# A hybrid decoder step on one core: gate and row loads on another queue, the merged sum added by an accumulating load, the last columns cut 384/160

## The chip, the core and the metric

One core of a Trainium2 chip runs the whole kernel. The metric is the device time of one execution in microseconds (us), the median of several runs. The profile is one execution taken by the hardware profiler; its times are us from the start of its span, unless marked ns. Engines: PE is TensorE (PEld its weight loads), DVE is VectorE, ACT is ScalarE, POOL is GpSimd, SP is the engine that does nothing here but issue DMAs. DMAs that ACT and POOL issue stand in those engines' own instruction order.

## What is computed

One layer of a decoder for 544 tokens (512 of a prompt, 32 of eight running requests). Three branches (short convolution, state-space, cross-attention) are projected to 2048 channels, gated, added and projected once more:

```
g = sigmoid(gpre).reshape(bsz, L, 3, D_MODEL)
conv_out = (cb * conv * silu(cz)) @ w_conv_out
ssm_out  = (ys @ w_glu_a) * sigmoid(ys @ w_glu_b)
attn_out = (o * silu(az)) @ w_attn_out
merged = g[:, :, 0] * conv_out + g[:, :, 1] * ssm_out + g[:, :, 2] * attn_out
y = rmsnorm(x + merged @ w_out) * final_norm_g
```

Everything is float32. Products are made in three matmuls of fp32r operands: each operand is split into a high part and a remainder, and hi·hi, hi·lo and lo·hi are accumulated.

## The kernel before

**Order.** The code is written for the Tile framework, whose planner puts each engine's instructions in an order by its own estimate of their times; so the order on an engine is not always that of the lines. Each engine then runs its list strictly in that order, and waits at the head of it.

**Weights.** A weight block of 512 KB (a "raw" tile) is loaded by SP. `split` makes its high part on ACT (L114, `whi`) and its remainder on DVE (L115, `wlo`), into a ring of pairs; the matmuls read the pair. `rings` sets the rings of a stage. `hold` is a tiny copy on POOL that reads the newest `wlo` (`ws["mark"]`) and writes the first element of a tile about to be loaded, so that the load is not issued earlier. `tick` runs one step of queued side work: first one entry of `later`, then steps of `bg`.

**Gate projections (to about 1546 us).** `winograd` makes products of the input projection by a seven-product scheme (order 1, 5, 6, 3, 7, 2, 4) from the factors `XT[1]` to `XT[7]` of the normed input, each 1088 KB for the high and 1088 KB for the low part. `XT[4]`, `XT[5]`, `XT[6]` are loaded by POOL at L1042 to L1044, right after the attention output has been stored by ACT (`od_d<-o_all`, L1031), and `XT[7]` at L1078. The first blocks of this stage's additional weight ring (`srw`) lie where `o_all` lay.

**Branch projections (about 1546 to 1917 us).** `winograd2` does the same for three output matrices with the factor sets `fsets` (`bh`, `bl`), four column groups `q` each: attention, convolution, then `w_glu_a` and `w_glu_b` in turn; 16 groups of seven products of 24 matmuls. Four raw tiles feed a group; `s1 = a21 + a22` (L1243, `bsum`) needs the third of them early. The ring of raw tiles has six slots (four `wraw`, two `bxr`), that of split pairs three. `gate` loads the group's two gate tiles (`sgate`, 544 KB each, two buffers) on SP, issued after the group's raw tiles. The gated results are stored by POOL to `mg_d` (L1285, L1296): the first branch plainly, the second and the third with an accumulating store that adds to what lies in DRAM.

**Handover and output projection (1917 us to the end).** Eight tiles `mgt` of the merged sum are read back by POOL (L1308) through two buffers, and split into 16 pairs `mh`, `ml` of 128 channels. The rows of x for the residual (`yt`, 4.46 MB in all) are loaded by POOL at the same place (L1325). Then seven column blocks of 256 go through `proj` (L172, L175, L178); after each, `residual` transposes the result on PE, adds it to `yt` (DVE), squares it (ACT) and multiplies by the norm's gain (POOL). The eighth block is made for tokens 0 to 271 first and then for 272 to 543 (L1381 to L1389), with `residual` and `finish` for row tiles 0, 1 and then 2, 3, 4. `finish` computes the norm, scales a row tile (2048 columns, on DVE or ACT) and stores it: two DMAs of SP for tiles 0 to 3, four of ACT for tile 4 (32 rows).

Of the kernel before, what the change touches and what calls it, by code (L numbers as in the profile page):

```python
# [7 lines left out]
F32 = mybir.dt.float32  # L8
# [19 lines left out]
def hybrid_step_kernel(  # L28
# [12 lines left out]
    with ctx:  # L41
# [1145 lines left out]

        frs = ExitStack()
        fsets = []
        for i in (1, 0):  # L1190
            pool = frs.enter_context(tc.tile_pool(name=f"fset{i}", bufs=1, side="right", reuse_waits="tile"))
# [19 lines left out]

        def winograd2(w, col0, F, before=None):

# [5 lines left out]
            a11, a12, a21, a22 = blk[0, 0], blk[0, 1], blk[1, 0], blk[1, 1]  # L1219
            if before:  # L1220
                before()

# [49 lines left out]
        def run(g):  # L1272
            for _ in g:
                pass

        rate[0] = 1
        for br, w, F, nxt in ((2, w_attn_out[0], fsets[0], 1), (0, w_conv_out[0], fsets[1], 2)):
            for q in range(4):
                o = winograd2(w, q * 512, F, (lambda: run(load_factors(F, fd[0], False))) if (br, q) == (2, 0) else None)
                if not q:  # L1280
                    bg.append(load_factors(fsets[nxt % 2], fd[nxt]))
                sg = gate(br, q)
# [15 lines left out]
        frs.close()  # L1298


        rings()
        open_std()
        mhp = ctx.enter_context(tc.tile_pool(name="mhp", bufs=1, side="right", reuse_waits="tile"))
        mh = [mhp.tile([128, T], F32R, name=f"mh{j}") for j in range(16)]
        ml = [mhp.tile([128, T], F32R, name=f"ml{j}") for j in range(16)]
# [5 lines left out]
        brs.close()  # L1311
        ytp = ctx.enter_context(tc.tile_pool(name="ytp", bufs=1, side="right", reuse_waits="tile"))
# [36 lines left out]

        def finish(tiles):  # L1350
            for i in tiles:
                rows = rows_of(i)
                ss = small.tile([128, 1], F32, name="ss")
                V.reduce_sum(out=ss[:rows], in_=ssp[:rows, i, :], axis=AX.X)
                r = rstd_of(ss, rows)
                if i % 2:
                    S.mul(yt[i][:rows], yt[i][:rows], r[:rows, 0:1])
                else:
                    V.tensor_scalar(yt[i][:rows], yt[i][:rows], r[:rows, 0:1], None, op0=ALU.mult)
                if i < 4:  # L1360
                    for s in range(2):
                        nc.sync.dma_start(out=yp_v[2 * i + s], in_=yt[i][64 * s:64 * s + 64])
                else:
                    for l in range(4):
                        S.dma_start(out=ys_o[l], in_=yt[i][8 * l:8 * l + 8])
# [11 lines left out]
        oT = [fin.tile([128, T], F32, name="oT", bufs=4) for _ in range(2)]  # L1377
        for n in range(2):
            for m in range(2):
                for blk, hi, lo in blocks:  # L1380
                    for q in range(4):  # L1381
                        kt = blk * 4 + q
                        lh = hi[:, q, m * 128:(m + 1) * 128]
                        ll = lo[:, q, m * 128:(m + 1) * 128]
                        o = ps[m][:, n, :NH]
                        nc.tensor.matmul(o, lh, mrh(kt, n), start=(kt == 0), stop=False)
                        nc.tensor.matmul(o, lh, mrl(kt, n), start=False, stop=False)
                        nc.tensor.matmul(o, ll, mrh(kt, n), start=False, stop=(kt == 15))
                (S.copy if m else V.tensor_copy)(oT[m][:, n * NH:(n + 1) * NH], ps[m][:, n, :NH])  # L1389
            tiles = ((0, 1), (2, 3, 4))[n]  # L1390
            residual(7, tiles, oT)
            finish(tiles)

# [33 lines left out]
```

## Time and profile before

| | us |
|---|---|
| median of 3 runs | 2165.47 |
| lowest, highest | 2164.09, 2172.06 |
| the profiled execution's own time | 2164.23 |
| span of its profile | 2161.8 |
| PE busy in the span | 2068.0 |
| DVE, ACT, POOL busy | 1284.9, 809.9, 439.5 |

The span is divided by its stages: what a stretch has in PE busy time, how many matmuls it holds, and which clock PE was granted. A PE busy share near 1 at a full clock cannot be shortened by moving loads; a stretch below it can. The profiled execution lasted 2.4 us longer than its span, and 1.2 us less than the median.

### The profile page before, as it was taken

To read this page: it belongs to the slowest core of one execution; us is meant where nothing else is said; L and a number is where in the kernel's file an instruction comes from. 1 tells how busy PE (TensorE), PEld (TensorE's weight loads), DVE (VectorE), ACT (ScalarE), POOL (GpSimd) and SP (SyncE) were. 2 spreads that over 40 slices of the span, in tenths; PEclk is the share of its full clock that TensorE was granted. 3 is DMA by queue.
4 is the path that set the end of the run, shared out by engine and by line. 5 is a ranking of instruction groups with operands and counts; after the bars stand their busy time and mean duration, and the time that the engine had idled before them with its cause. 6 is when DMAs were issued, how large, how long until landed. Compare 5 with 4: busy or idle time off the path is not lost.

```text
span 2161.8 us, 38757 instructions
## 1 busy us (share of the span) xinstructions
PE 2068.0 (96%) x16122; PEld 2016.1 (93%) x16122; DVE 1284.9 (59%) x1877; ACT 809.9 (37%) x1153; POOL 439.5 (20%) x518
## 2 busy tenths in 40 slices
PE   7999999999999999989999999999999899969996
PEld 5899999999999998879999999999899899969996
DVE  6664367943134743238887877767587686753232
ACT  6622222122122433224555555444444344433232
POOL 1008970054201102110121111000121100021121
PEclk9999999999999999999999999999999999989998
DMA  8747612234344626486677776643697955474223
GB/s 261 224 156 143 126 59 90 89 116 108 99 118 146 182 90 224 173 299 172 198 241 221 212 214 207 181 129 110 217 345 252 293 142 164 144 184 137 88 89 83
DMA packets 341619, 363.59 MB, mean 168 GB/s; under 512 B 62507, under 2 KB 288387, under 8 KB 338661
## 3 DMA queue, kind: packets, MB, share of 16 engines
q1 hardware_dynamic: 263712, 211.19, 33.2%
q0 software_dynamic: 38960, 118.48, 17.7%
q10 hardware_dynamic: 38772, 31.46, 5.0%
q8 instruction: 126, 2.06, 0.4%
q14 instruction: 49, 0.39, 0.1%
HBM read 280.82 MB, written 79.73 MB: 167 GB/s over the span
## 4 chain that ended last, share of the span: by engine, by line
PE 80%; DMA 7%; DVE 5%; POOL 2%; issue 2%; ACT 1%; ACTq 1%; DVEq 0%; SPq 0%; POOLq 0%
PE pA L1103 14%; PE pB L1103 11%; PE mmps L172 11%; PE mmps L178 11%; PE mmps L175 11%; PE pbA L1232 5%; PE pbB L1232 4%; DMA raw<-in_w_glu_b_dram 2%; DVE wlo L115 2%; DMA mgt<-mg_d 1%; PE mmps L324 1%; PE mmps L323 1%; PE mmps L325 1%; DMA raw<-in_w_in_dram 1%; DMA bl<-fd 1%
## 5 line engine op out<-in xcount | busy, mean ns | idle before, releaser
L115 DVE TENSOR_TENSOR wlo<-raw,whi 128x1024 fp32r<-128x1024 f32 x395 | 505.9, 1282 | 462.9 <-ACT whi L114 456.0
L114 ACT ACTIVATE whi<-raw 128x1024 fp32r<-128x1024 f32 x395 | 418.5, 1060 | 836.4 <-PE mmps L175 406.0
L172 PE MATMUL mmps<-xh,whi 128*128 128x272 f32 x1856 | 390.3, 291 | 1.5 <-ACT whi L114 1.3
L175 PE MATMUL mmps<-xl,whi 128*128 128x272 f32 x1856 | 389.6, 289 | 0.0
L178 PE MATMUL mmps<-xh,wlo 128*128 128x272 f32 x1856 | 386.7, 289 | 1.1 <-DVE wlo L115 1.1
L175 PEld LDWEIGHTS mmps<-xl,whi 128*128 128x128 f32 x1856 | 293.7, 188 | 4.3 <-issue 4.1
L172 PEld LDWEIGHTS mmps<-xh,whi 128*128 128x128 f32 x1856 | 290.9, 188 | 6.9 <-issue 4.5
L178 PEld LDWEIGHTS mmps<-xh,wlo 128*128 128x128 f32 x1856 | 290.9, 188 | 5.0 <-issue 2.7
L1232 PE MATMUL pbA<-bh,whi 128*128 128x272 f32 x512 | 149.5, 292 | 6.6 <-DVE bo L1256 5.0
L1232 PE MATMUL pbA<-bl,whi 128*128 128x272 f32 x512 | 149.1, 292 | 1.8 <-DMA bl<-fd 1.8
L1232 PE MATMUL pbA<-bh,wlo 128*128 128x272 f32 x512 | 148.9, 292 | 0.0
L1103 PE MATMUL pB<-xh,whi 128*128 128x272 f32 x432 | 126.2, 292 | 3.1 <-ACT whi L114 3.1
L1103 PE MATMUL pB<-xh,wlo 128*128 128x272 f32 x432 | 125.7, 291 | 0.0
L1232 PE MATMUL pbB<-bh,wlo 128*128 128x272 f32 x384 | 113.8, 296 | 12.0 <-DVE wlo L115 12.0
L1103 PE MATMUL pB<-xl,whi 128*128 128x272 f32 x432 | 125.3, 290 | 0.0
L1103 PE MATMUL pA<-xth,whi 128*128 128x272 f32 x432 | 124.4, 288 | 0.7 <-DVE sgate L1124 0.6
L1103 PE MATMUL pA<-xh,wlo 128*128 128x272 f32 x432 | 124.8, 289 | 0.0
L1103 PE MATMUL pA<-xh,whi 128*128 128x272 f32 x432 | 124.7, 289 | 0.0
L1103 PE MATMUL pA<-xth,wlo 128*128 128x272 f32 x432 | 124.6, 288 | 0.0
L1103 PE MATMUL pA<-xl,whi 128*128 128x272 f32 x432 | 124.4, 288 | 0.0
L1103 PE MATMUL pA<-xtl,whi 128*128 128x272 f32 x432 | 124.1, 287 | 0.0
L172 PE MATMUL mmps<-mh,whi 128*128 128x272 f32 x448 | 93.9, 294 | 21.0 <-ACT mh L114 21.0
(402 smaller groups left out, 4595.2 us busy)
## 6 DMA issues: line engine op xcount, KB each, us to landing
raw<-in_w_in_dram SPq DMA_DIRECT2D x224, 512.0 KB, 3.9
fd<-fs POOLq DMA_DIRECT2D x84, 272.0 KB, 4.0
raw<-in_w_out_dram SPq DMA_DIRECT2D x32, 512.0 KB, 3.4
gt_d<-sgate ACTq DMA_DIRECT2D x24, 544.0 KB, 3.1
sgate<-gt_d SPq DMA_DIRECT2D x24, 544.0 KB, 7.1
mg_d<-bo POOLq DMA_DIRECT2D x24, 544.0 KB, 8.4
bh<-fd POOLq DMA_DIRECT2D x21, 544.0 KB, 7.7
bl<-fd POOLq DMA_DIRECT2D x21, 544.0 KB, 9.0
```

Of the source, the lines that this page charges most:

```text
L114: S.activation(hi, src, AF.Copy)
L115: V.tensor_sub(lo, src, hi.bitcast(F32))
L172: nc.tensor.matmul(ps[m][:, n, :NH], lh, rh(kt, n), start=(kt == 0), stop=False)
L175: nc.tensor.matmul(ps[m][:, n, :NH], lh, rl(kt, n), start=False, stop=False)
L178: nc.tensor.matmul(ps[m][:, n, :NH], ll, rh(kt, n), start=False, stop=(kt == nk - 1))
L323: nc.tensor.matmul(o, lh, hi[:, q, :], start=(kt == 0), stop=False)
L324: nc.tensor.matmul(o, lh, lo[:, q, :], start=False, stop=False)
L325: nc.tensor.matmul(o, ll, hi[:, q, :], start=False, stop=(kt == 15))
L1103: nc.tensor.matmul(ps, a[:, k, :], t[:, k, :], start=new and i == 0, stop=i == 23, skip_group_check=not new)
L1232: nc.tensor.matmul(ps[:, s], a[:, k, s * 128:(s + 1) * 128], t[:, k, :], start=new and i == 0, stop=i == 11, skip_group_check=not new)
```

## The change

Five edits. The input factors are loaded as 5, 6, then 7 (as soon as its place is free), then 4, the last one held until the newest weight split. The gate tiles are loaded by POOL ahead of the group, no longer by SP behind its weights. The two `mgt` buffers are dropped and the raw ring of the branch projections gets two more slots, eight in all. The third branch is no longer stored: an accumulating load adds `mg_d` into the result tile in SBUF, and the split into `mh`, `ml` follows in later ticks, into memory of the factor set that is no longer used; the last tile is split after the last group. The row loads come after the first column block, and each `residual` runs one block later. The last column block is made for tokens 0 to 383 first, then for 160; `finish` follows for tiles 0, 1, 2 and then 3, 4, these scaled in two halves, one on DVE and one on ACT, and tile 3 stored in halves.

```diff
-        for n in (5, 6, 4):
+        def load_xt(n):
             for hl in range(2):
                 P.dma_start(out=XT[n][hl], in_=xf_d[n][hl])
+        load_xt(5)
+        load_xt(6)
...
-        for hl in range(2):
-            P.dma_start(out=XT[7][hl], in_=xf_d[7][hl])
+        load_xt(7)
+        for t in XT[4]:
+            hold(t[:, 0, 0:1])
+        load_xt(4)
...
-        mtp = brs.enter_context(tc.tile_pool(name="mgt", bufs=2, reuse_waits="tile"))
-        bxr = bps.enter_context(tc.tile_pool(name="bxr", bufs=2, reuse_waits="tile"))
-        rings([bxr] * 2, [bxh])
+        bxr = bps.enter_context(tc.tile_pool(name="bxr", bufs=4, reuse_waits="tile"))
+        rings([bxr] * 4, [bxh])
...
             for i in range(2):
-                nc.sync.dma_start(out=sg[i], in_=gt_d[br, 2 * q + i])
+                P.dma_start(out=sg[i], in_=gt_d[br, 2 * q + i])
...
-                o = winograd2(w, q * 512, F, (lambda: run(load_factors(F, fd[0], False))) if (br, q) == (2, 0) else None)
+                if (br, q) == (2, 0):
+                    for _ in load_factors(F, fd[0], False):
+                        pass
+                sg = gate(br, q)
+                o = winograd2(w, q * 512, F)
...
+        mh, ml = [], []
+        for pair in fsets[1].values():
+            for t in pair:
+                t = t.rearrange("p k t -> p (k t)")
+                mh.append(t[:, :T])
+                ml.append(t[:, T:])
+        def merged(t, k0):
+            for j in range(2):
+                split(mh[k0 + j], ml[k0 + j], t[:, j])
         for q in range(4):
+            sg = gate(1, q)
             o = winograd2(w_glu_a[0], q * 512, fsets[0])
-            sg = gate(1, q)
...
-                P.dma_start(out=mg_d[2 * q + i], in_=o[i], accum_op=ALU.add)
+                P.dma_start(out=o[i], in_=mg_d[2 * q + i], accum_op=ALU.add)
+                if (q, i) != (3, 1):
+                    later.append(lambda t=o[i], k0=4 * q + 2 * i: merged(t, k0))
+        flush()
+        merged(o[1], 14)
...
-        for i in range(8):
-            t = mtp.tile([128, 2, T], F32, name="mgt")
-            P.dma_start(out=t, in_=mg_d[i])
-            for j in range(2):
-                split(mh[2 * i + j], ml[2 * i + j], t[:, j])
...
-        for i in range(5):
-            hold(yt[i][:, 0:1])
-            load_rows(yt[i], i, P)
...
-            residual(jp, range(5), oT)
+            if not jp:
+                for i in range(5):
+                    hold(yt[i][:, 0:1])
+                    load_rows(yt[i], i, P)
+            else:
+                residual(jp - 1, range(5), prev)
+            prev = oT
+        residual(6, range(5), prev)
...
-        for n in range(2):
+        for n, (c0, c1) in enumerate(((0, 384), (384, T))):
...
-            tiles = ((0, 1), (2, 3, 4))[n]
-            residual(7, tiles, oT)
-            finish(tiles)
+            if n:
+                residual(7, (3, 4), oT)
+                finish((3, 4), True)
+            else:
+                residual(7, (0, 1, 2), oT)
+                finish((0, 1, 2))
```

## Rows read from the trace of the kernel before

**Rows 1.** The page's first line and the clock that PE was granted, in 40 equal slices of the span (tenths of full speed).

```profile
span 2161.8 us, 38757 instructions
PEclk9999999999999999999999999999999999989998
```

**Rows 2.** Busy time in six stretches. Columns: stretch, its length, then for PE, PEld, DVE, ACT and POOL the busy us (and instructions), the granted clock as a share of full speed, the DMA engines' busy share, GB/s.

```profile
1566.00:1676.00 110.00, 110.00 (x881) 110.00 (x880) 90.28 (x84) 48.22 (x56) 21.76 (x50) 1.00 0.91 301
1676.00:1917.00 241.00, 223.58 (x1709) 221.84 (x1707) 172.42 (x161) 102.49 (x118) 21.14 (x39) 0.96 0.60 178
1917.00:1962.00 45.00, 24.40 (x170) 23.16 (x171) 15.77 (x20) 14.20 (x22) 9.77 (x17) 0.81 0.94 245
1962.00:2117.00 155.00, 154.80 (x1238) 154.17 (x1237) 45.73 (x59) 48.24 (x101) 28.12 (x30) 1.00 0.25 84
2117.00:2143.00 26.00, 25.98 (x210) 25.65 (x207) 6.26 (x22) 8.03 (x21) 5.00 (x7) 1.00 0.13 30
2143.00:2162.00 19.00, 0.55 (x3) 0.27 (x3) 6.17 (x23) 3.81 (x11) 2.08 (x3) 0.60 0.69 194
```

**Rows 3.** PE's waits over the span: who waited for whom, us in total, times, longest.

```profile
PE mmps L172 <- ACT mh L114: 21.0, 4, 16.9
PE pbB L1232 <- DVE wlo L115: 12.0, 5, 4.0
PE pB L1103 <- ACT whi L114: 11.8, 5, 8.7
PE pbA L1232 <- DVE bo L1256: 5.0, 2, 4.4
```

**Rows 4.** What SP's own queue waited for from 1676 to 1917 us: us in total, times, longest.

```profile
SPq L1217 <- DVE wlo L115: 139.5, 34, 10.5
SPq L1269 <- DVE bo L1295: 27.1, 6, 8.3
SPq L1269 <- DVE bo L1284: 19.5, 6, 6.1
```

**Rows 5.** DVE's waits from 1545 to 1920 us, in the same columns.

```profile
DVE bsum L1243 <- DMA raw<-in_w_glu_b_dram: 25.1, 4, 7.7
```

**Rows 6.** SP's queue in order of time around the second `w_glu_b` group: start, us, what.

```profile
1768.89 2.53 SPq L1217 DMA_DIRECT2D raw<-in_w_glu_b_dram  x2
1779.80 0.34 SPq L1269 DMA_DIRECT2D sgate<-gt_d  x1
1780.93 0.37 SPq L1217 DMA_DIRECT2D raw<-in_w_glu_b_dram  x1
...
1786.08 0.37 SPq L1217 DMA_DIRECT2D raw<-in_w_glu_b_dram  x1
```

**Rows 7.** Instructions in order of time at the end of the first `w_glu_b` group: ACT's copy of the group's last product, and POOL's two accumulating stores.

```profile
1778.75 0.59 ACT L1262 COPY bo<-pbA 128x544 f32<-128x544 f32 x1
...
1780.06 0.85 POOL L1296 DMA_DIRECT2D mg_d<-bo  x1 [40.94 <-DVE bo L1295]
1782.40 0.85 POOL L1296 DMA_DIRECT2D mg_d<-bo  x1 [1.49 <-DVE bo L1295]
```

**Rows 8.** Those two stores, and the two around the handover (1910 to 1930 us): issues with KB each and us from issue to landing, then the least, median and greatest landing time of the handover's.

```profile
mg_d<-bo POOLq DMA_DIRECT2D x1, 544.0 KB, 8.4
mg_d<-bo POOLq DMA_DIRECT2D x1, 544.0 KB, 10.2
DMA to landing us min/median/max: 14.7/18.1/18.5
```

**Rows 9.** DVE's groups by shape from 1676 to 1917 us, and the remainders of the merged sum from 1917 to 1965 us: busy us, mean ns of one, idle before.

```profile
L115 DVE TENSOR_TENSOR wlo<-raw,whi 128x1024 fp32r<-128x1024 f32 x51 | 62.3, 1221 | 16.0 <-ACT whi L114 16.0
L1247 DVE TENSOR_TENSOR raw<-raw 128x1024 f32<-128x1024 f32 x9 | 11.0, 1219 | 0.0
L1256 DVE TENSOR_TENSOR bo<-pbA,bo 128x544 f32<-128x544 f32 x10 | 7.2, 721 | 4.2 <-PE pbA L1232 4.2
L1295 DVE TENSOR_TENSOR bo<-bo,sgate 128x1088 f32<-128x1088 f32 x7 | 9.0, 1286 | 1.2 <-ACT bo L1294 1.2
L115 DVE TENSOR_TENSOR ml<-mgt,mh 128x544 fp32r<-128x544 f32 x16 | 10.8, 722 | 26.4 <-ACT mh L114 26.4
```

**Rows 10.** ACT in order of time at the handover, and two groups of DMA issues from 1917 to 1962 us (KB each, median us to landing).

```profile
1941.44 1.20 ACT L114 ACTIVATE mh<-mgt 128x544 fp32r<-128x544 f32 x2 [15.34 <-DMA mgt<-mg_d]
...
yt<-in_x_prompt_dram POOLq DMA_DIRECT2D x3, 512.0 KB, 18.8
```

**Rows 11.** The input factors: SP's waits from 925 to 1005 us, and the landing times (least, median, greatest) of the three high and the three low loads of L1044.

```profile
SPq L1090 <- DMA od_d<-o_all: 21.3, 4, 12.1
...
DMA to landing us min/median/max: 7.2/13.8/19.9
...
DMA to landing us min/median/max: 9.9/16.8/23.0
```

**Rows 12.** Matmuls of other widths. Two of 512 columns in order of time (nine starts apart), four transposes of 128 columns in the chain that ended last, and a group of 72 columns in plain float32 (busy us, mean ns).

```profile
59.77 0.39 PE L324 MATMUL mmps<-wlo,mth 128*128 128x512 f32 x1
...
61.81 0.39 PE L324 MATMUL mmps<-wlo,mth 128*128 128x512 f32 x1
...
2117.01 0.44 PE aux L1342 x4
...
L717 PE MATMUL aux<-Sb,pw 128*128 128x72 f32 x128 | 28.3, 310 | 0.0
```

**Rows 13.** The end, in order of time: the first store of an output tile, the scaling of tile 2 (DVE) and of tile 3 (ACT), the four stores of tile 4 (ACT), and the DMA total from 2134 to 2162 us.

```profile
2138.53 1.17 SPq L1362 DMA_DIRECT2D out_dram<-yt  x2
...
2147.07 1.28 DVE L1359 TENSOR_SCALAR yt<-yt,rstd 128x2048 f32<-128x2048 f32 x1
2147.23 2.00 ACT L1357 ACTIVATE yt<-yt,rstd 128x2048 f32<-128x2048 f32 x1 [1.32 <-DVE rstd L216]
2149.99 6.99 ACTq L1365 DMA_DIRECT2D out_dram<-yt  x4
...
DMA packets 704, 4.46 MB, mean 159 GB/s; under 512 B 160, under 2 KB 160, under 8 KB 160
```

More of the change, by code (lines that the diff above doesn't have):

```diff
@@ L1184, in hybrid_step_kernel @@
         xs.close()
-        frs = ExitStack()
+        frs = [ExitStack(), ExitStack()]
+        ctx.callback(frs[1].close)
         fsets = []
         for i in (1, 0):
-            pool = frs.enter_context(tc.tile_pool(name=f"fset{i}", bufs=1, side="right", reuse_waits="tile"))
+            pool = frs[i].enter_context(tc.tile_pool(name=f"fset{i}", bufs=1, side="right", reuse_waits="tile"))
             fsets.insert(0, {n: tuple(pool.tile([128, 4, NH], F32R, name=f"b{hl}{n}_{i}") for hl in "hl")
                              for n in (4, 2, 7, 3, 6, 5, 1)})
-        mtp = brs.enter_context(tc.tile_pool(name="mgt", bufs=2, reuse_waits="tile"))
         bps = ExitStack()
@@ L1210, in load_factors, with winograd2 @@
                 yield
-        def winograd2(w, col0, F, before=None):
+        def winograd2(w, col0, F):
             blk = {}
@@ L1219, in winograd2 @@
             a11, a12, a21, a22 = blk[0, 0], blk[0, 1], blk[1, 0], blk[1, 1]
-            if before:
-                before()
             def product(ps, n, src, new):
@@ L1268, in gate @@
             for i in range(2):
-                nc.sync.dma_start(out=sg[i], in_=gt_d[br, 2 * q + i])
+                P.dma_start(out=sg[i], in_=gt_d[br, 2 * q + i])
             return sg
-        def run(g):
-            for _ in g:
-                pass
         rate[0] = 1
@@ L1278, in hybrid_step_kernel @@
             for q in range(4):
-                o = winograd2(w, q * 512, F, (lambda: run(load_factors(F, fd[0], False))) if (br, q) == (2, 0) else None)
+                if (br, q) == (2, 0):
[3 more added lines that the diff above has]
+                o = winograd2(w, q * 512, F)
                 if not q:
                     bg.append(load_factors(fsets[nxt % 2], fd[nxt]))
-                sg = gate(br, q)
                 for i in range(2):
@@ L1295, in hybrid_step_kernel @@
                 V.tensor_mul(o[i], o[i], sg[i])
-                P.dma_start(out=mg_d[2 * q + i], in_=o[i], accum_op=ALU.add)
+                P.dma_start(out=o[i], in_=mg_d[2 * q + i], accum_op=ALU.add)
+                if (q, i) != (3, 1):
+                    later.append(lambda t=o[i], k0=4 * q + 2 * i: merged(t, k0))
+        frs[0].close()
+        mhx = ctx.enter_context(tc.tile_pool(name="mhx", bufs=2, side="right", reuse_waits="tile"))
+        for j in range(2):
+            mh.append(mhx.tile([128, T], F32R, name="mhx"))
+            ml.append(mhx.tile([128, T], F32R, name="mlx"))
+        flush()
+        merged(o[1], 14)
         bps.close()
-        frs.close()
+        brs.close()
         rings()
         open_std()
-        mhp = ctx.enter_context(tc.tile_pool(name="mhp", bufs=1, side="right", reuse_waits="tile"))
-        mh = [mhp.tile([128, T], F32R, name=f"mh{j}") for j in range(16)]
-        ml = [mhp.tile([128, T], F32R, name=f"ml{j}") for j in range(16)]
-        for i in range(8):
-            t = mtp.tile([128, 2, T], F32, name="mgt")
-            P.dma_start(out=t, in_=mg_d[i])
-            for j in range(2):
-                split(mh[2 * i + j], ml[2 * i + j], t[:, j])
-        brs.close()
         ytp = ctx.enter_context(tc.tile_pool(name="ytp", bufs=1, side="right", reuse_waits="tile"))
@@ L1348, in residual, with finish @@
                 P.tensor_mul(yv, yv, fg[:rows, jp * 256:(jp + 1) * 256])
-        def finish(tiles):
+        def finish(tiles, halves=False):
+            rs = {}
             for i in tiles:
@@ L1354, in finish @@
                 V.reduce_sum(out=ss[:rows], in_=ssp[:rows, i, :], axis=AX.X)
[L1355 to L1363, printed above, removed]
+                rs[i] = rstd_of(ss, rows)
+            for i in tiles:
+                rows, r = rows_of(i), rs[i]
+                y = yt[i][:rows]
+                h = D // 2 if halves else D
+                for c, on_act in (((0, False), (h, True)) if halves else ((0, i % 2),)):
+                    if on_act:
+                        S.mul(y[:, c:c + h], y[:, c:c + h], r[:rows, 0:1])
+                    else:
+                        V.tensor_scalar(y[:, c:c + h], y[:, c:c + h], r[:rows, 0:1], None, op0=ALU.mult)
+                    if i < 4:
+                        for s in range(2):
+                            nc.sync.dma_start(out=yp_v[2 * i + s][:, c:c + h], in_=y[64 * s:64 * s + 64, c:c + h])
+                if i == 4:
                     for l in range(4):
-                        S.dma_start(out=ys_o[l], in_=yt[i][8 * l:8 * l + 8])
+                        S.dma_start(out=ys_o[l], in_=y[8 * l:8 * l + 8])
         for jp in range(7):
@@ L1377, in hybrid_step_kernel @@
         oT = [fin.tile([128, T], F32, name="oT", bufs=4) for _ in range(2)]
-        for n in range(2):
+        for n, (c0, c1) in enumerate(((0, 384), (384, T))):
             for m in range(2):
+                o = ps[m][:, n, :c1 - c0]
                 for blk, hi, lo in blocks:
@@ L1384, in hybrid_step_kernel @@
                         ll = lo[:, q, m * 128:(m + 1) * 128]
[L1385 to L1389, printed above, removed]
-            tiles = ((0, 1), (2, 3, 4))[n]
-            residual(7, tiles, oT)
-            finish(tiles)
+                        nc.tensor.matmul(o, lh, mh[kt][:, c0:c1], start=(kt == 0), stop=False)
+                        nc.tensor.matmul(o, lh, ml[kt][:, c0:c1], start=False, stop=False)
+                        nc.tensor.matmul(o, ll, mh[kt][:, c0:c1], start=False, stop=(kt == 15))
+                (S.copy if m else V.tensor_copy)(oT[m][:, c0:c1], o)
+            if n:
+                residual(7, (3, 4), oT)
+                finish((3, 4), True)
+            else:
+                residual(7, (0, 1, 2), oT)
+                finish((0, 1, 2))
 _INS = ['x_prompt', 'x_sample', 'mem_prompt', 'cache_mem_k', 'cache_mem_v', 'state_conv',
```

## The prediction

> **What bounds the kernel now.** I read the page first: over most of the span PE is granted its full clock, and the weak slices lie near the end [rows 1]. Then the stretches: from 1566 to 1676 us PE has work all the time, 881 matmuls in 110.0 us, 0.1249 us each, and again from 1962 to 2143 us. Two stretches fall short [rows 2]. From 1676 to 1917 us 1709 matmuls would take 213.4 us at that price; they take 241.0, so 27.6 us are lost, 17.4 of them as idle time and 10.2 to the lower granted clock (0.96 on average, so part of it at 1.2 GHz) that follows the gaps. From 1917 to 1962 us 170 matmuls would take 21.2 us and take 45.0: 23.8 us lost. After PE's last column block, 19 us of output follow. So the kernel is bound by PE, with 51.4 us that are someone else's.
>
> Whose, the waits tell. In the first stretch PE waits for DVE's weight remainders and for a copy [rows 3]; DVE in turn sat before `bsum`, 25.1 us for `w_glu_b` blocks alone [rows 5]; and those were late because SP had not issued them: its queue stood 46.6 us before gate loads whose buffers were still in use [rows 4]. The order of time shows it: two blocks of the next group go out at 1768.89, then SP stands before a gate load until 1779.80, and the third and fourth blocks follow at 1780.93 and 1786.08 [rows 6]. The 139.5 us before L1217 is a full ring of raw tiles, which is no loss by itself. In the second stretch PE waits 21.0 us for the merged sum's split [rows 3], ACT 15.34 us at once for an `mgt` load, which shares the DMA engines with the row loads (18.8 us to land) [rows 10].
>
> **The change part by part.**
>
> *Gate loads to POOL, eight raw slots.* The 24 gate issues leave SP, and with them all of the 46.6 us; a whole group of weights can lie ready. POOL takes them at about 0.85 us each [rows 7], 20 us in all, beside 21.14 busy us in a stretch of 241 [rows 2]. On POOL a gate load waits for the same release that the store of the last result waits for, so what is queued behind it (factor loads with their holds, the next store) loses little; the gate is used a group, 21 us, later. Removed: the 27.6 us. From below the bound is nothing, if DMA bandwidth and not the queue made the blocks late. I take the full removal, because the DMA engines are busy 0.60 of this stretch, against 0.91 in the one before it, where PE had no gap [rows 2].
>
> The Trainium skill speaks against this part: "DMA: Bandwidth & Descriptors", section "Issuing engines are not separate DMA queues", says that transfers run on the same 16 engines whichever engine issues them, so that spreading them only saves sequencer time. By that this term would be 0; the rows show a queue standing in order, not a shortage of engines. It is the second rival below.
>
> *Accumulating load and merged split in the ticks.* The load into SBUF stands in place of the accumulating store, which landed 8.4 and 10.2 us after issue [rows 8]. No row shows one into SBUF; I take those two, the nearest in kind, size and place. Above, the crowded handover's 18.5 us is the bound [rows 8]; below, nothing excludes that it lands at once, and then the stalls are none. New is a wait on ACT: the merged split stands in ACT's list between weight splits, and the next weight split is queued behind it, which PE waits for. Let T be the end of a group. The two loads go out at T+1.3 and T+3.7 [rows 7]. The second lands at T+13.9; two copies on ACT (1.2 us), then a weight split on ACT (about 1.1) and DVE (1.2), put the next weights at T+17.4, or T+landing+7.2. A product is 24 matmuls, 3.0 us; the sixth is due at T+15. That is a stall of 2.4 us; a landing of 8.4 us would make it 0.6. The copies of the first load stand in the way as well, so I take 2 us at each of the three transitions. DVE adds: a group has 7 splits of 1.22, 4 sums of 1.22, 3 additions of 0.72 and 2 gate products of 1.29 us, 18.2 us; four remainders of 0.72 make 21.1 in a group of 21.0 us [rows 9]. DVE is then full in three groups; I put 2 us on that in all. Stalls of 8 us; each idle us cost 0.59 us more by the clock in this stretch (10.2 over 17.4), so 12.7 us come back. Net: 27.6 - 12.7 = 14.9 saved. Bounds: 27.6, and 0 if every transition stalls 5 us.
>
> The same page, section "Anatomy of one DMA", has a fit of 2.0 us plus bytes over 436 GB/s, an estimate of 3.3 us for 544 KB; by it no merged split would be late and the sum would be some 10 us better. The stores measured 8.4 and 10.2, so it is not used.
>
> *Handover.* The eight `mgt` loads and 12 of the 16 splits leave it; the row loads move behind the first column block, where DMA is 0.25 busy and their first use is 25 us later [rows 2]. What is late next: the merged pairs 12 to 15. They belong to the fourth weight block of the first column block, due 18 us after the start; the loads land 10 to 14 us after it. The cost is again ACT's order: the third weight block may stand behind a merged split, some 2 us by the sum above, and 2 us for the start. Loss stood to idle time as 23.8 to 20.6 here, 1.16 [rows 2], so I keep 4.6 us and save 23.8 - 4.6 = 19.2; bounds 12 and 23.
>
> *Input factors.* The first blocks of the gate stage wait for the stores of `o_all`, whose place they take: SP stood 21.3 us for them [rows 11]. Those stores share the engines with POOL's loads. The new order sends 5, 6 and 7 at once and only then 4; the loads landed between 7.2 and 23.0 us after issue [rows 11], so number 7 is still under way when number 4 is released and POOL's queue never runs dry. The stores get the same share as now. I take 0; at best 3 us of the 8.7 us wait [rows 3], at worst 1. Behind the hold nothing urgent is queued on POOL.
>
> *Last block and tail.* 512 columns cost 0.227 us, nine starts in 2.04 us [rows 12], 272 cost 0.125, so 384 cost 0.173 by the line between them. 160 columns would be 0.077 by that line, but four transposes of 128 take 0.44, 0.11 each [rows 12]: I take 0.11, the row nearest in width. First part 96 × 0.173 = 16.6, second 96 × 0.11 = 10.6: 27.2 instead of 24.0 us. PE's end is not the end, though. Stores start at 2138.53 [rows 13], 8.5 us after the first part. The first part ends 4.6 us later than now, so stores begin near 2143.1; 4.46 MB at about 280 GB/s (they ran from 2138.5 to 2160 with gaps) take 15.9 us, so they end near 2159 to 2161, as before. The second part ends near 2146, its tile is scaled 6 us later in halves (0.65 on DVE, 1.0 on ACT instead of 2.00 [rows 13]), and its 1.3 MB join a stream still running. I take 0, from -3 to +3. The lagged residual moves 20 transposes per block by 25 us, past nothing that is short: PE has no idle time there [rows 2].
>
> **The sum.** 14.9 + 19.2 + 0 + 0 = 34.1 saved. From the profiled execution's 2164.2 that is 2130.1; against the median (1.2 higher) 2131. I say 2130.
>
> **The rivals.**
>
> *The merged load lands late (0.14).* At 12 us, each of four transitions stalls 12 - 7.8 = 4.2 us: 3 × 4.2 × 1.59 = 20.0, DVE 3.2, handover 7.2, in all 30.4 of the 51.4 come back: 2143. For it: no row has such a load; against it: without SP's burst behind each gate load these moments are emptier.
>
> *Queue order was not the cause (0.07).* If the blocks are late because the engines are shared, the first stretch keeps its loss, and only the handover gains: 2164.2 - 19.2 = 2145.
>
> *Narrow matmuls are dear (0.10).* The 72-column group took 28.3 us for 128, 0.22 each, in plain float32 and from strided data [rows 12]; by its price per column 160 columns would cost 0.49. Halfway, at 0.27 to 0.30, the second part takes 27 us, 16 more, of which stores hide 3: 2143.
>
> *Slower than before (0.05).* The merged load again, at its worst: each us of landing over 7.8 costs 3 × 1.59 + 1.16 = 5.9 us over the four transitions. With 5.5 fixed, the 51.4 saved are gone at a landing of 15.5 us, and 10.8 more at 17.4. The crowded handover had 14.7 to 18.5 [rows 8]; at 18.5 us it gives 2182. Against it: that crowd was the row loads, which move away.
>
> *It does not do what it says (0.04).* The planner's order may put the gate loads late on POOL, or merged splits before most weight splits, so that the old waits return under new names: about 2158.
>
> **How the numbers follow.** The forecast has 0.60. If nearly all of the 51.4 us goes and the tail and factors gain 3 us each at most, and a little stalls, the low end is 2112. The high end takes in three rivals with their spread: 2152. Left out are the last two rivals and the edges, about 0.15. A measurement here can tell about 0.5%, 10.8 us. Forecast and the first three rivals are faster by more than that, less a part of the first: 0.89. Within it: 0.07. Slower: 0.04.
>
> **What would show it.** SP's queue should have no wait for a gate's release, and `bsum` no wait for a block. From the convolution groups on, PE idle under 10 us. ACT waits for the accumulating loads, if they are late, stand at the first products of the second, third and fourth `w_glu_a` group. The handover's first `proj` should run within 5 us of full pace. The 160-column matmuls should start every 0.11 us. I am wrong if these loads land above 12 us, if PE's idle time is replaced by waits for DVE, or if the stores end over 3 us later after PE than I have them.

## The result, and the profile after

The changed kernel takes 2113.03 us (median of 4 runs, 2109.7 to 2114.6), the kernel before 2165.24 beside it: a ratio of 0.975, 95% interval 0.9726 to 0.9775. 52 us are gone where the forecast had 34: the direction was right, the size 17 us short of the 2130. By the medians the time is 1 us above the low end of the range (2112); by the ratio, from the 2165.47 that the prediction started from, it is 2111.3, just below it. The profiled execution took 2109.7 us, its span is 2107.8. The experiments below were timed in four rounds, each beside the kernel before, whose medians there lie between 2163.87 and 2166.03; so a difference between kernels of two rounds is good to some 2 us.

The title's "another queue" holds for the gate loads alone: the row loads stay on POOL and go out later. It leaves out two edits that turn out to pay, the two raw slots and the order of the input factors.

The page after: its first line, the granted clock in 40 slices, and the head of the chain that ended last; the weak slices of [rows 1] are gone but for the last.

```profile
span 2107.8 us, 38720 instructions
PEclk9999999999999999999999999999999999999998
...
PE 82%; DMA 5%; issue 5%; POOL 3%; DVE 3%; ACTq 1%; ACT 1%; POOLq 0%; SPq 0%; DVEq 0%
```

Stretches of the kernel after, in the columns of [rows 2]: the branch groups, the handover, the last block, the rest of the output.

```profile
1669.00:1886.00 217.00, 215.56 (x1719) 215.02 (x1718) 181.20 (x173) 110.11 (x131) 24.26 (x41) 1.00 0.63 188
1886.00:1931.00 45.00, 45.00 (x361) 45.00 (x361) 13.47 (x13) 12.59 (x16) 8.98 (x19) 1.00 0.93 233
...
2059.00:2089.00 30.00, 30.00 (x217) 29.75 (x215) 10.05 (x35) 10.45 (x33) 9.20 (x13) 1.00 0.06 13
2089.00:2108.00 19.00, 0.88 (x6) 0.32 (x5) 4.02 (x16) 3.79 (x9) 1.39 (x2) 0.60 0.74 216
```

In the branch groups PE idles 1.4 us where 17.4 were idle, and its clock is full; in the handover it idles not at all. Waits of the kernel after, from 1545 to 1920 us, that answer to [rows 3 to 5] (us in total, times, longest): PE's largest, then SP's own queue, then DVE's longest for a block.

```profile
PE pbA L1236 <- DVE wlo L115: 1.3, 1, 1.3
...
SPq L1223 <- DVE wlo L115: 250.8, 52, 12.4
...
DVE bsum L1247 <- DMA raw<-in_w_glu_a_dram: 6.1, 1, 6.1
```

The waits for a gate's release are gone from SP's queue. That fits the prediction, and is not the cause, as E2, E6 and E13 show.

**Where the time went** is read from three starts in each trace: that of the last matmul into `pB` (end of the gate projections), of the last into `pbA` (end of the branches), and of the first of the last column block. Before: 1542.8, 1916.3, 2117.2, span end 2161.8. After: 1535.7, 1884.3, 2059.5, 2107.8. The differences give four stretches (us), which every experiment has too (its time is the median of its own runs):

| kernel | time, us | to end of projections | branches | handover and 7 blocks | last block and output |
|---|---|---|---|---|---|
| before | 2165.24 | 1542.8 | 373.5 | 200.9 | 44.6 |
| after | 2113.03 | 1535.7 | 348.6 | 175.2 | 48.3 |
| E1 before, new input order | 2155.44 | 1540.0 | 372.9 | 199.3 | 44.4 |
| E2 before, gates on POOL | 2163.41 | 1546.8 | 374.8 | 201.1 | 44.5 |
| E3 after, old input order | 2121.93 | 1543.6 | 348.6 | 175.2 | 48.4 |
| E4 after, 272/272 | 2111.85 | 1536.0 | 350.9 | 175.2 | 45.5 |
| E5 after, six slots | 2137.86 | 1537.1 | 376.7 | 175.2 | 48.1 |
| E6 after, gates on SP | 2115.12 | 1538.3 | 353.9 | 175.2 | 47.6 |
| E7 after, merge twice | 2132.17 | 1538.2 | 356.9 | 185.2 | 48.7 |
| E8 after, store and reload | 2147.56 | 1537.9 | 350.5 | 210.6 | 48.3 |
| E9 before, wider rows | 2174.63 | 1546.2 | 379.4 | 204.3 | 44.5 |
| E10 after, wider rows | 2116.14 | 1540.9 | 347.9 | 175.2 | 47.9 |
| E11 after, wider rows for 6 | 2110.79 | 1536.7 | 348.1 | 175.2 | 48.5 |
| E12 after, row loads early | 2121.83 | 1535.4 | 347.7 | 184.4 | 48.5 |
| E13 before, eight slots | 2146.84 | 1544.9 | 348.4 | 208.8 | 45.0 |
| E14 after, seven slots | 2116.28 | 1538.7 | 352.4 | 175.2 | 48.5 |
| E15 E11, 272/272, halves | 2107.05 | 1536.6 | 349.5 | 175.1 | 44.3 |

The first stretch scatters by up to 4 us between profiles of kernels that do the same there (1542.8, 1546.8 and 1544.9 in before, E2 and E13), most of it ahead of the first input load, which goes out at 938.9 us in before and between 940.4 and 943.0 in all the others. From before to after the four give -7.1, -24.9, -25.7 and +3.7: -54.0, the difference of the two spans. The forecast had 0, -14.9, -19.2 and 0.

### The profile page after: what moved, and what is told of

The parts are those of the page before. It is cut to its first block, busy times and chain, and to the rows that moved or that the text cites. A ratio compares the mean times of both kernels' runs of the same rounds, so it can differ in the third digit from the quotient of the medians.

```text
span 2107.8 us, 38720 instructions
## 1 busy us (share of the span) xinstructions
PE 2056.4 (98%) x16122; PEld 2006.9 (95%) x16122; DVE 1284.3 (61%) x1878; ACT 809.3 (38%) x1154; POOL 447.1 (21%) x536
## 4 chain that ended last, share of the span: by engine, by line
PE 82%; DMA 5%; issue 5%; POOL 3%; DVE 3%; ACTq 1%; ACT 1%; POOLq 0%; SPq 0%; DVEq 0%
PE pA L1109 12%; PE mmps L172 12%; PE mmps L178 12%; PE mmps L175 12%; PE pB L1109 10%; PE pbA L1236 8%; PE pbB L1236 5%; DVE wlo L115 1%; DMA bl<-fd 1%; PE mmps L324 1%; PE mmps L323 1%; PE mmps L325 1%; DMA raw<-in_w_glu_a_dram 1%; PE aux L717 1%; DMA raw<-in_w_in_dram 1%
## 5 line engine op out<-in xcount | busy, mean ns | idle before, releaser
L1236 PE MATMUL pbB<-bl,whi 128*128 128x272 f32 x384 | 110.7, 288 | 1.2 <-DMA bl<-fd 1.2
```

The lines of the kernel that those rows point to most:

```text
L1236: nc.tensor.matmul(ps[:, s], a[:, k, s * 128:(s + 1) * 128], t[:, k, :], start=new and i == 0, stop=i == 11, skip_group_check=not new)
```

## Experiments on the branches: queue or slots

**E2, the gate loads alone.** The kernel before with

```diff
-                nc.sync.dma_start(out=sg[i], in_=gt_d[br, 2 * q + i])
+                P.dma_start(out=sg[i], in_=gt_d[br, 2 * q + i])
```

and `sg = gate(...)` ahead of the group's weights.

> The kernel before with the gate loads issued by POOL ahead of their group's weights; the ring of raw tiles stays at six slots, and the merged sum stays an accumulating store that is loaded again at the handover. Theory of the queue (SP standing before gate loads was the whole loss of the stage): the time between the last gate projection and the last branch matmul falls by 20 to 25 us, to about 2142. Rival, the two more ring slots did it: a gain under 8 us, 2157 or more, with waits of bsum for raw blocks left. Rival, shared engines (the queue that issues does not matter): no gain, 2164.

2163.41 us, ratio 0.9985 (0.997 to 1.0001); the branches take 374.8 us, as before. The prediction's queue theory falls. Waits of E2, SP's queue and DVE, from 1545 to 1920 us, and three instructions around one `w_glu_b` group in order of time: the remainder that freed a slot, SP's issue of the group's third block into it, and the sum that waited for that block.

```profile
SPq L1217 <- DVE wlo L115: 314.8, 58, 15.2
...
DVE bsum L1243 <- DMA raw<-in_w_glu_b_dram: 25.1, 4, 6.9
...
1784.71 1.22 DVE L115 TENSOR_TENSOR wlo<-raw,whi 128x1024 fp32r<-128x1024 f32 x1
...
1785.96 0.37 SPq L1217 DMA_DIRECT2D raw<-in_w_glu_b_dram  x1
...
1796.91 1.23 DVE L1243 TENSOR_TENSOR bsum<-raw 128x1024 f32<-128x1024 f32 x1 [5.83 <-DMA raw<-in_w_glu_b_dram]
```

SP no longer stands before gate loads, and stands longer before L1217 instead. The third block goes out when a remainder of the group at work has released its slot. It then takes 10.8 us to land, beside the stores and gate loads that go out within 3 us of it, where the group's first two took 4.5 and 4.7. `bsum`, which adds the second block and the third, waits 25.1 us in all for `w_glu_b` blocks, the very number of [rows 5]. How much of that a quicker landing alone would save, no run shows.

**E5, six slots in the changed kernel.**

```diff
-        bxr = bps.enter_context(tc.tile_pool(name="bxr", bufs=4, reuse_waits="tile"))
+        bxr = bps.enter_context(tc.tile_pool(name="bxr", bufs=2, reuse_waits="tile"))
```

and `rings([bxr] * 2, [bxh])`.

> The changed kernel with six raw slots instead of eight. E2 has put SP's standing before gate loads in doubt. Theory of slots (with six slots the third and fourth block of a group go out only when blocks of the group at work are released, and then land too late; a wait before a full ring is the loss): the stage between the last gate projection and the last branch matmul takes some 25 us more again, about 2138, with bsum waiting 25 us or more for raw blocks. Theory of the queue, as predicted: under 8 us more, about 2113 to 2121.

2137.86 us, 24.8 more than the changed kernel; the branches take 376.7. DVE's longest wait and PE's, in E5 from 1545 to 1920 and from 1560 to 2000 us:

```profile
DVE bsum L1247 <- DMA raw<-in_w_glu_b_dram: 26.8, 4, 7.6
...
PE pbB L1236 <- DVE wlo L115: 20.9, 5, 5.4
```

Both rows of the kernel before are back [rows 3, 5], with the gate loads on POOL.

**E6, the gate loads back on SP** behind the weights of their group, eight slots kept.

> The changed kernel with its gate loads on SP again, behind the weights of their group; eight slots stay. Theory of slots: little changes, 2113 to 2118, for with all four blocks out ahead SP may stand before a gate load for 10 us without harm. Theory of the queue: most of the 25 us of the stage come back, 2130 to 2138.

2115.12 us, 2.1 more. In E6 (SP's queue and DVE, 1545 to 1920 us)

```profile
SPq L1273 <- DVE bo L1287: 61.8, 16, 9.9
SPq L1273 <- DVE bo L1311: 26.6, 6, 8.3
...
DVE bsum L1247 <- DMA raw<-in_w_glu_a_dram: 0.2, 1, 0.2
```

SP stands 88.4 us before gate loads whose buffers are in use, and no sum waits more than 0.2 us for a block: with four blocks out ahead this standing is nearly harmless. It costs 2.1 us by the time, 5.3 by the branches' row of this profile, and nothing in that row of E13, whose gates are on SP as well.

**E13, eight slots and nothing else.** The changed kernel with gates, merged part, row loads, input order and last block put back; the two `mgt` buffers, for which there is no room beside eight slots, get their place after the branches.

> The kernel before with eight raw slots and nothing else of the change in effect: gates on SP behind the weights, accumulating stores, the reload through two buffers (which now get their place only after the last branch matmul), row loads, order of the transformed inputs and last block as before. Theory of slots: the branch stage gives back 25 us, and the reload costs up to 8 us more than before for its later place: 2140 to 2149. If the slots need the other queue or the merged part to be of use: 2158 or more.

2146.84 us, ratio 0.992 (0.9904 to 0.9937). The branches take 348.4 us, all of the changed kernel's gain, and the handover 7.9 us more than before, as priced. So the slots alone are the cause of the 25 us, and what the merged part gives this stage is the room for them.

**E14, seven slots** (`bufs=3` and `* 3`).

> The changed kernel with seven raw slots. Theory of slots: with seven, one block of a group instead of two goes out late, and it is the fourth, which the third of the sums needs, not the first; so a step well between: 3 to 12 us more than the changed kernel, 2116 to 2125. If landing times are what counts and eight is just enough: near 2138, as with six. If seven are enough: 2113.

2116.28 us, 3.3 more, 3.8 in the branches' row. From six slots (E5) to eight it is 24.8 us by the time and 28.1 by that row; the seventh slot brings 21.6 and 24.3 of them, and the eighth the rest, which is little more than the scatter. That it is the fourth block which then comes late was only argued; DVE's one wait over 1 us for a block there is 6.9 us, for a convolution block.

## Experiments on the input factors: who gets the DMA engines

**E1 and E3, the order of the loads**, alone on the kernel before, and undone in the changed one. E1's edit is the diff's first two hunks.

> The kernel before with the new order of the transformed inputs alone (numbers 5, 6, 7 and then the held 4); nothing else changes. The prediction's step (the stores of the attention result get the same share of the engines as before): no gain, 2164 within 2 us, SP's wait for those stores stays at 21 us. Theory of packets: queues take turns packet by packet, so the store with 2176-byte packets gains as soon as the load beside it has 1088-byte packets (number 7, into a strided place) instead of 8704-byte ones; then the store lands some 4 us earlier, SP's wait falls to about 17 us, PE's gap at the first gate blocks from 8.7 to about 4.7 us, and the time by 6 to 9 us, to about 2157.

> The changed kernel with the old order of the transformed inputs (5, 6, 4 at once, 7 later); the rest is as changed. Theory of packets: the 7 to 9 us come back, about 2121, with PE's gap at the first gate blocks near 8.7 us again. The prediction's step: within 2 us of the changed kernel's 2113.

E1: 2155.44 us, ratio 0.9946 (0.993 to 0.9963), which is 11.7 us of before's 2166.03; E3: 2121.93, 8.9 more than the changed kernel. The edit is worth 9 to 12 us, not 0. In the traces the stretch from the first input load to the end of the projections takes 602.0 to 604.0 us with the old order (before, E2, E3, E13), 597.6 in E1, and 594.1 to 596.7 in the changed kernel and the seven others with its input loads (E4 to E8, E12, E14): some 6 to 9 us. The rows that show why are the DMA queues: packets, MB, share of the engines. q0 is POOL's (the input loads), q10 ACT's (the stores of `o_all`), q1 SP's (weight blocks). The kernel before from 942 to 950 us, 3 us after the first input load is issued; then the kernel after from 952 to 960 us, when the load of number 7 joins:

```profile
q0 software_dynamic: 328, 2.58, 80.3%
q10 hardware_dynamic: 328, 0.64, 23.7%
...
q0 software_dynamic: 420, 2.03, 67.2%
q10 hardware_dynamic: 422, 0.82, 26.4%
q1 hardware_dynamic: 418, 0.21, 13.1%
```

In these two windows the queues move equal numbers of packets, so bytes follow packet size: 2.58 MB / 328 is 7.9 KB (numbers 5, 6 and 4 move rows of 8704 bytes), 0.64 MB / 328 is 2.0 KB. Number 7 goes into a strided place in rows of 1088 bytes. The new order brings it to the engines earlier, the stores end earlier, and SP's wait, which was 21.3 us [rows 11], and PE's gap, which was 8.7 us [rows 3], shrink; in E3 they are back at 21.1 and 8.8. The kernel after, SP's wait and PE's from 925 to 1005 us:

```profile
SPq L1096 <- DMA od_d<-o_all: 17.1, 4, 10.2
...
PE pB L1109 <- ACT whi L114: 4.7, 1, 4.7
```

The Trainium skill has a rule for this in "DMA: Bandwidth & Descriptors", section "Queues, rings and completion order": each engine goes round the queues that have work, a packet at a time. The rows above agree (328 and 328; 420, 422 and 418), those of E9 below do not go one for one; the price in us is from the runs.

**E9, packet size alone.** The kernel before, order unchanged, with

```diff
-            XT[n] = tuple(xtp.tile([128, 8, NH], F32R, name=f"xt{hl}{n}") for hl in "hl")
+            XT[n] = tuple(xtp.tile([128, 8, NH + 4], F32R, name=f"xt{hl}{n}")[:, :, :NH] for hl in "hl")
```

> The kernel before, loads, order and bytes unchanged, but the tiles of the transformed inputs 4, 5 and 6 get rows of 276 elements instead of 272, of which 272 are used: their loads then move 1088-byte pieces into a strided place, as the load of number 7 does, instead of 8704-byte ones. Theory of packets: beside them the stores of the attention result get a larger share, land 4 us or more earlier, SP waits 10 to 17 us for them instead of 21, and the time falls by 6 to 12 us, to 2154 to 2160, with no change of order at all. Rival, order and bytes set it (the later load of number 4 frees the engines): no gain, 2165.

2174.63 us, ratio 1.0045 (1.003 to 1.0061): 10 us more, where the theory had 6 to 12 less. The queues of E9 from 945 to 953 us (again 3 us after the first input load), SP's wait for the stores, and PE's longest:

```profile
q0 software_dynamic: 1256, 1.35, 70.5%
q10 hardware_dynamic: 625, 1.21, 47.1%
...
SPq L1090 <- DMA od_d<-o_all: 8.6, 4, 4.2
...
PE pA L1103 <- DMA xh<-xf: 10.7, 1, 10.7
```

The direction is there: with the order untouched the stores move 1.21 MB instead of 0.64, SP waits 8.6 us instead of 21.3. But the input loads now pay: number 7, last in the queue, takes 41.2 us to land instead of 29.4, and PE waits 10.7 us for it. From the first input load to the end of the projections it is 604.1 us, no better than with the old order: what the stores gained is lost again, and the expectation failed on what is late next. That is not the 10 us, though. In the profile they stand in stretches that the edit was not meant to touch: the branches take 379.4 us and the handover 204.3, 5.9 and 3.4 more than in the kernel before, and `bsum` waits 15.6 us for attention blocks where it waited 6.4. Why the wider rows do that stays open.

**E10 and E11, the same in the changed kernel**, for 4, 5 and 6, and for 6 alone.

> The changed kernel with the same rows of 276 elements for 4, 5 and 6. Theory of packets: the stores land earlier still, PE's gap of 4.7 us at the first gate blocks shrinks, 3 to 8 us less, 2105 to 2110. Rival, the slower loads of 5 and 6 become what PE waits for, or the gap is held by something else than the stores: 2113 or more.

> The changed kernel with rows of 276 elements for number 6 alone; 5 and 4 as changed. Between the changed kernel and E10: if the share follows packets, the stores gain while 6 is under way, 1 to 5 us less, 2108 to 2112; by the rival 2113.

E10: 2116.14 us, 3.1 more; SP waits 8.5 us for the stores, and PE 3.5 us for number 7 and 2.6 for one of the others: the rival's kind, though the longer wait is for a load that it did not name. E11: 2110.79, ratio 0.9757 (0.9732 to 0.9781), not to be told from the changed kernel, though SP's wait falls to 13.0. PE's waits from 925 to 1005 us are 5.7 us in all there and 5.6 in the changed kernel: they have only moved.

## Experiments on the merged sum and the handover

**E7, each accumulating load made twice.**

```diff
-                P.dma_start(out=o[i], in_=mg_d[2 * q + i], accum_op=ALU.add)
+                for _ in range(2):
+                    P.dma_start(out=o[i], in_=mg_d[2 * q + i], accum_op=ALU.add)
```

> The changed kernel with every accumulating load of the merged sum made twice (so the stored sum is added twice, and the output is another). The second lands about 8 us after the first, which moves the merged split's due time by that. The prediction's price, 5.9 us per us of landing over 7.8: some 47 us more, about 2160. Theory of slack (the planner's list leaves ACT 5 us or more before a merged split stops a weight split, and each idle us costs little): 10 to 30 us more, 2123 to 2143. If landing is hidden anyway: 2113.

2132.17 us, 19.1 more. ACT in order of time at the first transition, where PE waited 0.2 us in the kernel after: first the kernel after, then E7, whose loads went out 1.2 us later.

```profile
1765.88 0.67 ACT L114 ACTIVATE bh<-bo 128x544 fp32r<-128x544 f32 x1 [0.52 <-DMA bo<-mg_d]
...
1766.99 1.05 ACT L114 ACTIVATE whi<-raw 128x1024 fp32r<-128x1024 f32 x1
...
1772.20 0.66 ACT L114 ACTIVATE bh<-bo 128x544 fp32r<-128x544 f32 x1 [3.66 <-DMA bo<-mg_d]
```

```profile
1778.43 0.66 ACT L114 ACTIVATE bh<-bo 128x544 fp32r<-128x544 f32 x1 [6.34 <-DMA bo<-mg_d]
...
1781.68 0.66 ACT L114 ACTIVATE bh<-bo 128x544 fp32r<-128x544 f32 x1
```

The second split starts at 1772.20 after and at 1781.68 in E7, 8.3 us later but for the 1.2. Counted from the issue of a group's first load, the last one lands 8.2, 8.8 and 9.8 us later than after at the three transitions and 14.0 us later at the handover. For that the branches pay 8.3 us over three transitions and the handover 10.0 (table), 18.3 in all, where the prediction's price for 8 us was 47. That is 0.7 us per us at the handover (prediction 1.16) and 0.3 at a transition (1.59). Part of the reason is order: in E7 the planner puts two weight splits more ahead of the first merged one, so the run prices a later landing together with the order made for it.

**E8, the merged part undone**: `accum_op` in a store to `mg_d`, then eight loads through two `mgt` buffers and their splits.

> The changed kernel with the merged part undone: the third branch is added by an accumulating store, the sum is loaded through two buffers after the last branch matmul and split there; ring, gate queue, row loads and tail stay as changed. If that reload is the handover's loss, of which the prediction put 23.8 us to it and the row loads together: 15 to 20 us more, 2128 to 2133. If the row loads beside it were the cause: under 8 us more, 2121 or less.

2147.56 us, 34.5 more, 35.4 in the handover's column: above both expectations. POOL in order of time, and ACT's wait, in E8:

```profile
1914.86 3.05 POOL L255 DMA_DIRECT2D yt<-in_x_prompt_dram  x6 [0.97 <-issue]
...
1921.69 0.56 POOL L1322 DMA_DIRECT2D mgt<-mg_d  x1 [2.97 <-DMA yt<-in_x_prompt_dram]
...
ACT mhx L114 <- DMA mgt<-mg_d: 24.9, 1, 24.9
```

The last reload went out behind the row loads and took 20.6 us to land; PE stood 23.5 us for it. So the run does not part reload and crowd: both are in it.

**E12, the row loads before the first column block again.**

> The changed kernel with the row loads ahead of the first column block again, where the kernel before had them. If the crowd of row loads was what made the handover's landings late: the last accumulating loads and the first weight blocks of the projection land late and 5 to 15 us come back, 2118 to 2128. If the reload through two buffers was the cause and the place of the row loads is worth nothing: 2111 to 2115.

2121.83 us, 8.8 more, 9.2 of it in the handover. DMA issues of E12 from 1884 to 1940 us (the accumulating load's median landing; it was 6.3 in the kernel after), and PE's wait:

```profile
bo<-mg_d POOLq DMA_DIRECT2D x2, 544.0 KB, 18.2
...
PE mmps L172 <- ACT mhx L114: 5.5, 1, 5.5
```

So of the handover's 25.7 us, 9 hang on the place of the row loads. The rest is left to the merged part, but no run puts the reload back as the kernel before had it (E8 and E13 reload later), so its own worth stays open.

## Experiments on the last block

**E4, 272/272 again**, tiles 0 and 1 first, then 2, 3 and 4 whole; **E15**, E11 with 272/272 and the later tiles in halves.

```diff
-        for n, (c0, c1) in enumerate(((0, 384), (384, T))):
+        for n, (c0, c1) in enumerate(((0, 272), (272, T))):
```

> The changed kernel with the last column block cut 272/272 again, tiles 0 and 1 finished after the first part and 2, 3 and 4 after the second, whole. The account by anchors says that the new cut cost 3.8 us after the start of the last block: about 2109. The prediction's step (nothing is gained or lost): 2113. If 384/160 does help: 2116.

> The changed kernel with rows of 276 elements for the transformed input 6 and with the last block cut 272/272, the later tiles (2, 3, 4) scaled in halves. If the small gains seen in E4 (1 us) and E11 (2 us) are real and add up: 2108 to 2110. If they were noise: 2113.

E4: 2111.85 us, ratio 0.975 (0.9733 to 0.9767), the changed kernel's own ratio. E15: 2107.05, ratio 0.974 (0.9725 to 0.9754): the lowest time of all, and not surely below the changed kernel's by the intervals. The last column tells more than the times: 47.6 to 48.7 us in all ten profiles with 384/160, 45.5 in E4, 44.3 in E15. Against these two the new cut costs 2.8 and 4.0 us. E4's time doesn't show it (in its profile the branches were 2.3 us longer); E15's does, 3.7 us below E11's, a difference of two rounds. SP's stores in order of time, after and E4, begin at

```profile
2086.41 15.22 SPq L1381 DMA_DIRECT2D out_dram<-yt  x10
```

```profile
2083.97 15.19 SPq L1381 DMA_DIRECT2D out_dram<-yt  x8
```

that is 26.9 and 21.9 us after the block's first matmul, and the output then ends 21.4 and 23.6 us later: the wider first part holds the stores back by 5 us, and the smaller second part gives only 2.2 of them back.

## Why the prediction came out 17 us short

**The ring stage: cause wrong, size of the loss right.** "Removed: the 27.6 us" held, but not for the queue. The step that failed is the reading of the wait before L1217: "a full ring of raw tiles, which is no loss by itself". A full ring was the loss: two of a group's four blocks could not be sent for ahead. The rows had it: DVE sat before `bsum` for blocks [rows 5], and the third and fourth went out only at 1780.93 and 1786.08 [rows 6]; both the gate load and a slot held them back, and the slot came last. DVE's remainders of the group at work, in the kernel before, show it, and then the sum that waited:

```profile
1779.69 1.22 DVE L115 TENSOR_TENSOR wlo<-raw,whi 128x1024 fp32r<-128x1024 f32 x1
...
1784.83 1.23 DVE L115 TENSOR_TENSOR wlo<-raw,whi 128x1024 fp32r<-128x1024 f32 x1 [1.59 <-ACT whi L114]
1793.73 1.22 DVE L1243 TENSOR_TENSOR bsum<-raw 128x1024 f32<-128x1024 f32 x1 [7.68 <-DMA raw<-in_w_glu_b_dram]
```

The remainders end at 1780.91 and 1786.06, each 0.02 us before an issue. The length of the wait is not the sign (with eight slots it is 250.8 us and costs nothing); which block it holds is. That the size came out right was luck as far as the queue goes, since the slots stood in the same edit; the signs that the prediction named for this stage (no wait for a gate's release, PE idle under 10 us) came true for the same reason, and could not tell the queue from the slots. The rival that the queue was not the cause had the first half right (E2), and its 2145 wrong, for the slots again. The Trainium skill's "DMA: Bandwidth & Descriptors", section "Issuing engines are not separate DMA queues", would have had 0 for the queue. E2 agrees, with 2.6 us and an interval that reaches 1.

**What comes back, 12.7 us: mis-sized.** The second load of a transition, which sets the stall, landed 9.0 to 9.7 us after its issue, little sooner than the 10.2 taken; the landing did not make the difference. What failed is "the sixth is due at T+15". The weight split behind the second merged split belongs to the seventh product, one product later. In the kernel after, at the first transition (T is 1758.81), ACT's split, DVE's remainder and PE's first matmul of that product:

```profile
1773.32 1.99 ACT L114 ACTIVATE whi<-raw 128x1024 fp32r<-128x1024 f32 x2
...
1774.39 1.23 DVE L115 TENSOR_TENSOR wlo<-raw,whi 128x1024 fp32r<-128x1024 f32 x1
...
1775.72 0.29 PE L1236 MATMUL pbA<-bh,whi 128*128 128x272 f32 x1
```

The weights are ready at T+16.8, where the sum had T+17.4, and that is just in time. So PE idled 1.4 us in the stage after, its clock stayed at full speed, and DVE, full by the sum, was busy at most 37.5 us of the 42 that two groups take (the four remainders come once in two groups): 24.9 saved, not 14.9.

**Handover, 4.6 us kept: mis-sized.** Nothing was left; PE ran without a gap. 25.7 saved, of which about 0.7 is six transposes that the lag moved into the last block (22 there instead of 16, 0.11 us each [rows 12]; a block has ten, not the prediction's 20).

**Input factors, 0: wrong.** The step was "The stores get the same share as now". The stores' share rose when the loads beside them had smaller packets (1:1 by packets in the two windows above, 1:2 in E9), and the order of the loads changes whose packets stand beside the stores: 7.1 us in the table, 9.4 from the first input load on, 9 to 12 in timed runs.

**Last block, 0 from -3 to +3: +3.7.** The 160 columns, seven starts apart in the kernel after, in order of time:

```profile
2078.25 0.28 PE L1414 MATMUL mmps<-bh,wlo 128*128 128x160 f32 x1
...
2079.03 0.28 PE L1412 MATMUL mmps<-bl,whi 128*128 128x160 f32 x1
```

That is 0.111 us each, as taken from the transposes, so the rival of dear narrow matmuls is out. What failed is the stores' time. The sum had them begin 4.6 us later and take 15.9 us, at 280 GB/s. They began 5.6 us later (26.9 us after the block's first matmul, 21.3 before), 0.7 of it by the moved transposes, and the output ended 21.4 us after that, only 1.9 sooner than the 23.3 before.

The misses add up: 7.1 + 10.0 + 6.5 - 3.7 = 19.9, and 54.0 - 34.1 = 19.9. The rival of a merged load at its worst decided at a landing of 15.5 us. E12 shows that the crowd can bring it to 18.2 us at the handover; it paid 9.2 us there, where 1.16 for each us over 7.8 makes 12.1.

## What to carry to other kernels

When a queue stands before two kinds of instruction, ask of each wait what would still hold the late transfer if that wait were gone: here a ring two slots short held it, and took over the 25 us unchanged. Space is a cause too: the edit that paid was the one that freed room for two slots. When transfers share the engines, compare their packet sizes before assuming equal shares, and look at what is last in the queue of the one that loses.

## What was not expected of the hardware

Two DMA queues beside each other moved 328 packets each in 8 us, 2.58 MB against 0.64. With 1088-byte packets on the first queue the second moved 1.21 MB, but with 625 packets against 1256; why not one for one there stays open. The whole rate fell from 406 to 320 GB/s. Matmuls of 160 columns started 0.111 us apart, hardly less than the 0.125 of 272 columns.
